# A mixture-of-experts layer on one core: its experts are worked two at a time, a wide one and a narrow one in turn

## The chip, the core and the metric

The kernel runs on one core of a Trainium2 chip. A core has a matrix engine (TensorE, PE), which multiplies a stationary operand of up to 128 x 128 (loaded by LDWEIGHTS, shown as PEld) with a moving one of up to 512 columns and adds up in PSUM; VectorE (DVE), ScalarE (ACT) and GpSimd (POOL) for elementwise work; and SyncE (SP), which here issues most DMAs. Sixteen DMA engines move data between DRAM and the on-chip memory SBUF. The metric is the device time of one execution in microseconds (us).

## What is computed

One layer over 1024 latent tokens of 1024 numbers, with a prefix of 256 context tokens: layer norm, a modulated branch of a state-space scan and window attention, a residual with layer norm, and a mixture of experts with a second residual and layer norm. The change lies in the experts. Each token goes to the 4 of 32 experts with the highest router value; an expert's rows are put through

```
def expert_block(args):
    xb, e = args
    gu = xb @ w_gate_up[e] + b_gate_up[e]          # 1024 x 2048
    glu, lin = jnp.split(gu, 2, axis=-1)
    glu = jnp.minimum(glu, SWIGLU_LIMIT)
    lin = jnp.clip(lin, -SWIGLU_LIMIT, SWIGLU_LIMIT)
    act = glu * jax.nn.sigmoid(SWIGLU_ALPHA * glu) * (lin + 1)
    return act @ w_down[e] + b_down[e]             # 1024 x 1024
```

and the result, times the token's gate, is added to the token's row. All is in float32; 12.6 MB of weights per expert come from DRAM.

## The kernel before, in words

Ahead of the experts the kernel ranks them by their number of rows (`ranks`, L1127). The expert of rank r gets room for `CAPS[r]` rows (L1059): 256 for the three fullest, then 240, 224, 208, four times 192, five times 160, and 128 for the other 17. Experts with more than 128 rows are *wide* and have two row blocks (`BLOCKS`), the 17 others are *narrow*. `ORDER` (L1061) takes ranks 0, 31, 1, 30, ..., so that a wide and a narrow expert alternate, down to the two last, 15 and 16, which are both narrow. Rows over the room would be done in a loop at the end (`rest`, L1707), which runs zero times here.

Each float32 product is made of three in a faster format (fp32r): a matrix is split into a high part (ACT copies it) and a low part (DVE subtracts), and high x high, low x high and high x low are added up. `Weights` (L1436) does this for the weights. An expert's weights come in 12 chunks of 1 MB, each as two halves with a DMA of their own (L1459, issued on SP) into one of 8 `raw` buffers (`P.ahead`); `prepare` copies each half to `wh` (ACT, L1476) and subtracts to `wl` (DVE, L1478). There are four pairs of split buffers, and the split runs three chunks ahead of PE, so the split of a step waits until PE has finished the chunk of the step before.

An expert is worked in 12 steps (`moe`, L1645), eight for the up projection and four for the down projection:

- `gather` fetches the expert's rows by an indirect DMA on POOL (L1240), with the lists that `places` (one-hot tables, DVE, L1182) and `slots` (small matmuls, L1198, and sums on DVE) made some steps before. `x_parts` (L1273) transposes four 128-column pieces of a block at a time on PE (`turn`, L1262) and splits them (`put`, L1269 and L1271) into `x`, of which there are two buffers.
- `up_wide` (L1333) has the weights stationary and the rows moving, so the result is already transposed; a chunk of 256 output columns takes two of the five PSUM accumulators (`K.mm`). `act_wide` (L1348) adds the bias, alternately for gate and linear columns, and writes `a` split.
- `up` (L1296), for narrow experts, has the rows stationary and 512 weight columns moving; two chunks make one accumulator, and after the second the bias is added by one more matmul (L1305): a stationary matrix `sel` of 64 rows that is one where the row is this expert's, times the table `K.bgu` of all experts' biases, 32 rows of high and 32 of low parts. `act` (L1317) makes the activation `um` in two halves; `turn` flips it (at steps 5 and 9, `TURN`) and `put` splits it into `a`.
- `down` (L1407) multiplies `a` with `w_down`: first the upper half of the rows of the weights for both halves of the output columns, then the lower half (`DOWN`, L1431). `store` (L1415) applies the gate (L1425) and adds the rows into `acc_d` by an indirect DMA on POOL (L1427), the first half of the columns at step 11 and the second at step 0 of the next expert.

In the loop the orders of PE, DVE and ACT are written out by hand: `tc.manual_schedule` keeps the instructions of its body in program order on each of them. `weave` takes turns among the jobs of a step: the last expert's store, this expert's activation, the next split, a part of the next expert's x. In each step come first the transposes of this step's x part and flip, then the woven jobs, then the products of the chunk (`main`). PSUM has eight buffers here: five accumulators, two for transposes (`K.tp`), one for the lists. A pool hands a buffer out anew when its last reader is done.

The lines that matter, from `moe`:

```
x = next(xs, None) if c in (1, 6, 7, 10) else None
cur.before(c)
weave(prev.store(1) if c == 0 and prev else None, cur.after(c), W.prepare(), x)
...
cur.main(c, W.ready.pop(0))
```

Of the kernel before, what the change touches and what calls it, by code (L numbers as in the profile page):

```python
# [8 lines left out]
F32 = mybir.dt.float32  # L9
# [10 lines left out]
D = 1024  # L20
# [1039 lines left out]
BLOCKS = {256: (128, 128), 240: (128, 112), 224: (128, 96), 208: (128, 80), 192: (128, 64), 160: (128, 32), 128: (128,), 64: (64,)}  # L1060
# [66 lines left out]
def ranks(tc, a, K):  # L1127
# [30 lines left out]
    v.tensor_copy(K.pick, K.pk.bitcast(F32))  # L1158
# [56 lines left out]
TURN = 5, 9  # L1215


class Expert:
# [4 lines left out]
    def __init__(self, tc, K, P, blocks, pick, lists, eid=None):  # L1223
        self.tc, self.nc, self.K, self.P, self.blocks, self.lists = tc, tc.nc, K, P, blocks, lists
        self.wide = len(blocks) == 2
        self.n = sum(blocks)
        self.pick = pick
        self.eid = eid
# [14 lines left out]
    def constants(self):  # L1243
        nc, P, K = self.nc, self.P, self.K
        if self.wide:
            nc.vector.tensor_scalar(self.bias[:, 8:16], self.bias[:, 8:16], 1.0, None, ALU.add)
        else:
            s = P.pk.tile([64, 256], F32R, tag="pk", name="pk")
            nc.vector.tensor_scalar(s, K.full, self.pick, None, ALU.mult)
            self.sel = s[:, 0:128] if self.n == 128 else s[:, 128:256]  # L1250

    def lo(self, b):

        return b * 128 + (256 if self.blocks[b] > 64 else self.blocks[b])
# [18 lines left out]
    def x_parts(self):  # L1273


        self.x = self.P.xt.tile([128, KT, 512], F32R, tag="x", name="x")
# [40 lines left out]
    def act(self, q):  # L1317
# [3 lines left out]
        x = self.whole(self.gu, nb, ("hg", "hu")[q])[0:nb]  # L1321
        t = P.tmp.tile([128, 512], F32, tag=("sg", "um")[q], name="t")[0:nb]
# [25 lines left out]
    def act_wide(self, c):  # L1348
# [4 lines left out]
        t = [P.tmp.tile([128, 512], F32, tag=("sg", "um")[q], name="t") for _ in range(2)]  # L1353
# [27 lines left out]
    def before(self, c):  # L1381
        if not self.wide and c in TURN:
            self.pt = self.turn(0, lambda i: self.um[0:self.n, i * 128:(i + 1) * 128])

    def after(self, c):

        if c == 1:
            self.a = self.P.at.tile([128, KT, 512], F32R, tag="a", name="a")
        if not self.wide and c in TURN:
            yield from self.put(self.a, TURN.index(c) * 4, 0, self.lo(0), self.pt)  # L1390
        if c == 11:
# [7 lines left out]
    def main(self, c, w):  # L1399
        if c >= 8:  # L1400
            self.down(c % 2, (c - 8) // 2 * 4, w)
# [29 lines left out]
DOWN = [("w_down", 4, k, c) for k in (0, 4) for c in (0, 512)]  # L1431
# [4 lines left out]
class Weights:  # L1436
# [133 lines left out]
def expert_consts(tc, a, K, late):  # L1570
    nc = tc.nc
    K.bgu = late.tile([64, 2 * D], F32R, name="bgu")
    K.full = late.tile([64, 256], F32, name="full")
    nc.gpsimd.memset(K.full, 1.0)
    nc.gpsimd.memset(K.full[:, 192:256], 0.0)
    br = K.wp.tile([128, KT, 256], F32, tag="raw", name="br").rearrange("p k n -> p (k n)")[0:64]
    for j in range(2):
        nc.sync.dma_start(out=br[j * 32:(j + 1) * 32], in_=a["b_gate_up"])
    nc.gpsimd.tensor_scalar(br[:, D:], br[:, D:], 1.0, 1.0, ALU.add, ALU.mult)
# [6 lines left out]
def moe(tc, a, K):  # L1586
    nc = tc.nc
    es = ExitStack()
    with es:
# [4 lines left out]
        with ExitStack() as st:  # L1594
            P = expert_pools(tc, a, K, st, True)
            W = Weights(tc, a, P)
            for r in ORDER:
                W.add(lambda r=r: expert_id(nc, K, r), CAPS[r] > 128)
# [3 lines left out]
            def expert_id(nc, K, r):  # L1602
                if r not in regs:
                    regs[r] = nc.sync.value_load((eid if P.ahead == 8 else K.eid)[0:1, r:r + 1], min_val=0, max_val=31)
# [12 lines left out]
            def start(i, ls):  # L1617
# [3 lines left out]
                e = Expert(tc, K, P, BLOCKS[CAPS[r]], K.pick[:, r:r + 1], ls, lambda: expert_id(nc, K, r))  # L1621
# [4 lines left out]
            with tc.manual_schedule(engines={mybir.EngineType.PE, mybir.EngineType.DVE, mybir.EngineType.Activation}):  # L1626
# [7 lines left out]
                P.ahead = 8  # L1634
# [5 lines left out]
                nxt = start(1, next(it))  # L1640
                weave(W.prepare())
                cur.constants()
            prev = None
            with tc.manual_schedule(engines={mybir.EngineType.PE, mybir.EngineType.DVE, mybir.EngineType.Activation}):
                for i in range(len(ORDER)):  # L1645
                    xs = iter(nxt.x_parts()) if nxt else iter(())
                    for c in range(12):
                        if c == 5:
                            ls = next(lists(i + 2, oh) or iter(()), None)
                        x = next(xs, None) if c in (1, 6, 7, 10) else None  # L1650
                        cur.before(c)
                        weave(prev.store(1) if c == 0 and prev else None, cur.after(c), W.prepare(), x)
                        if c == 2:
                            oh = place(i + 2)
                        if c == 8:
                            n2 = start(i + 2, ls)
                        if c == 10 and nxt:
                            nxt.constants()
                        cur.main(c, W.ready.pop(0))
                    prev, cur, nxt = cur, nxt, n2  # L1660
                weave(prev.store(1))
# [45 lines left out]
def rest(tc, a, K):  # L1707
    nc = tc.nc
    v = nc.vector
    with ExitStack() as es:  # L1710
# [4 lines left out]
        with tc.For_i(0, count, 1) as i:  # L1715
# [18 lines left out]
            pk = sm.tile([64, 1], F32, tag="pk", name="pk")  # L1734
            v.tensor_tensor(pk, K.route[0:64, 65:66], row[0:64, 33:34], ALU.is_equal)
            W = Weights(tc, a, P)
            W.add(eid)
# [6 lines left out]
            for c in range(12):  # L1744
                e.before(c)
                weave(e.after(c), W.prepare())
# [498 lines left out]
```

## Time and profile before

| | |
|---|---|
| Median of three runs | 2791.53 us (2789.71 to 2792.7) |
| Profiled execution | 2796.39 us, its span 2794.6 us |
| Mean granted TensorE clock | 0.943 of full speed |
| PE, PEld busy over the span | 2523.9 us (90%), 2123.3 us (76%) |
| DVE, ACT, POOL busy | 2234.2 us (80%), 1465.9 us (52%), 465.0 us (17%) |
| Read from DRAM, written | 551.76 MB, 76.57 MB |

The span runs from the first to the last instruction. The expert loop begins with the first product of an expert at 1149.5 us and ends with its last store at 2725.4 us. Matmuls overlap one another and their ends are modelled, so the sum of their durations says little; the step from one start to the next one's says what a product costs.

### The profile page before, as it was taken

To read this page: it belongs to the slowest core of one execution; us is meant where nothing else is said; L and a number is where in the kernel's file an instruction comes from. 1 tells how busy PE (TensorE), PEld (TensorE's weight loads), DVE (VectorE), ACT (ScalarE), POOL (GpSimd) and SP (SyncE) were. 2 spreads that over 40 slices of the span, in tenths; PEclk is the share of its full clock that TensorE was granted. 3 is DMA by queue.
4 is the path that set the end of the run, shared out by engine and by line. 5 is a ranking of instruction groups with operands and counts; after the bars stand their busy time and mean duration, and the time that the engine had idled before them with its cause. 6 is when DMAs were issued, how large, how long until landed. Compare 5 with 4: busy or idle time off the path is not lost. (4 is left out here: it accounts for less than half of the span.)

```text
span 2794.6 us, 41588 instructions
## 1 busy us (share of the span) xinstructions
PE 2523.9 (90%) x14030; PEld 2123.3 (76%) x14030; DVE 2234.2 (80%) x4306; ACT 1465.9 (52%) x2352; POOL 465.0 (17%) x303
## 2 busy tenths in 40 slices
PE   6799999978887877699999999999999999999990
PEld 1698887767686767588888888889888887888770
DVE  9636796347788887788878888888988899899995
ACT  0623113656555422455656666666666666666661
POOL 3200000034333243210110110110111011101113
PEclk8799999979998877699999999999999999999995
DMA  7434623554454463678979978988998999899983
GB/s 252 155 125 157 202 87 116 161 172 136 163 169 139 146 195 102 209 244 266 290 226 284 295 242 283 292 273 272 303 294 262 305 301 300 275 305 302 311 280 144
DMA packets 409674, 631.11 MB, mean 226 GB/s; under 512 B 36497, under 2 KB 215569, under 8 KB 408497
## 3 DMA queue, kind: packets, MB, share of 16 engines
q1 hardware_dynamic: 397152, 584.37, 63.8%
q0 software_dynamic: 11872, 42.47, 6.5%
q8 instruction: 112, 1.84, 0.3%
q10 hardware_dynamic: 432, 1.57, 0.2%
q14 instruction: 106, 0.86, 0.1%
HBM read 551.76 MB, written 76.57 MB: 225 GB/s over the span
## 5 line engine op out<-in xcount | busy, mean ns | idle before, releaser
L1478 DVE TENSOR_TENSOR wl<-raw,wh 128x1024 fp32r<-128x1024 f32 x768 | 920.8, 1219 | 163.4 <-ACT wh L1476 162.3
L1476 ACT ACTIVATE wh<-raw 128x1024 fp32r<-128x1024 f32 x768 | 790.3, 1052 | 246.5 <-PE dn L1294 87.9
L1344 PE MATMUL uw<-x,wh 128*128 128x320 f32 (+5 forms) x1920 | 581.3, 366 | 0.2 <-issue 0.2
L1345 PE MATMUL uw<-x,wl 128*128 128x192 f32 (+4 forms) x1920 | 501.4, 261 | 0.0
L1344 PEld LDWEIGHTS uw<-x,wh 128*128 128x128 f32 x1920 | 364.3, 190 | 24.0 <-issue 0.3
L1345 PEld LDWEIGHTS uw<-x,wl 128*128 128x128 f32 x1920 | 369.6, 193 | 0.5
L1291 PE MATMUL dn<-wh,a 128*128 128x512 f32 (+4 forms) x752 | 298.7, 397 | 0.0
L1292 PE MATMUL dn<-wl,a 128*128 128x512 f32 (+4 forms) x752 | 293.6, 390 | 0.0
L1427 POOL DMA_INDIRECT acc_d<-y,wi x47 | 120.4, 2562 | 958.3 <-DVE y L1425 816.3
L1294 PE MATMUL dn<-wh,a 128*128 128x512 f32 (+3 forms) x608 | 238.5, 392 | 0.6 <-DVE a L1271 0.6
L1291 PE MATMUL up<-wh,x 128*128 128x512 f32 x544 | 221.8, 408 | 0.0
L1294 PE MATMUL up<-wh,x 128*128 128x512 f32 x544 | 213.0, 392 | 0.0
L1292 PE MATMUL up<-wl,x 128*128 128x512 f32 x544 | 212.3, 390 | 0.0
L1356 ACT ACTIVATE t<-uw,bias 128x160 f32<-128x160 f32 (+5 forms) x240 | 98.6, 419 | 134.5 <-PE uw L1345 131.6
L1291 PEld LDWEIGHTS dn<-wh,a 128*128 128x128 f32 (+4 forms) x752 | 135.7, 180 | 37.8 <-issue 4.1
L1292 PEld LDWEIGHTS dn<-wl,a 128*128 128x128 f32 (+4 forms) x752 | 135.8, 181 | 33.9
L608 POOL TENSOR_SCALAR P<-P,su 128x640 f32<-128x640 f32 (+1 forms) x64 | 55.1, 874 | 608.0 <-DVE su L606 543.9
L1294 PEld LDWEIGHTS dn<-wh,a 128*128 128x128 f32 (+3 forms) x608 | 112.8, 186 | 28.4 <-DVE a L1271 2.7
L42 ACT ACTIVATE whi<-raw 128x2048 fp32r<-128x2048 f32 x38 | 72.8, 1917 | 112.9 <-PE mm L53 72.5
L1240 POOL DMA_INDIRECT x<-xm_d,ri x47 | 53.3, 1135 | 463.3 <-DVE L L1202 304.0
L1291 PEld LDWEIGHTS up<-wh,x 128*128 128x128 f32 x544 | 102.3, 188 | 27.4 <-issue 8.4
L1294 PEld LDWEIGHTS up<-wh,x 128*128 128x128 f32 x544 | 102.1, 188 | 22.4
(532 smaller groups left out, 5349.2 us busy)
## 6 DMA issues: line engine op xcount, KB each, us to landing
raw<-w_gate_up SPq DMA_DIRECT2D x512, 512.0 KB
raw<-w_down SPq DMA_DIRECT2D x256, 512.0 KB
mw<-w_mod SPq DMA_DIRECT2D x64, 256.0 KB
raw<-w_o SPq DMA_DIRECT2D x16, 1024.0 KB
raw<-w_in SPq DMA_DIRECT2D x13, 1024.0 KB
raw<-w_mod SPq DMA_DIRECT2D x8, 1024.0 KB
gate_d<-gs SPq DMA_DIRECT2D x16, 512.0 KB
raw<-w_att_out SPq DMA_DIRECT2D x8, 1024.0 KB
```

What stands on the lines that cost most here:

```text
L42: nc.scalar.activation(out=hi, in_=src, func=ACTF.Copy)
L608: nc.gpsimd.tensor_scalar(P[i][:, 0:nl + 256], P[i][:, 0:nl + 256], su[:, 0, i:i + 1], 1.0, ALU.mult, ALU.mult)
L1240: nc.gpsimd.indirect_dma_start(out=x[0:nb], out_offset=None, in_=K.xm_d, bounds_check=S - 1, oob_is_err=True, in_offset=bass.IndirectOffse ...
L1291: nc.tensor.matmul(ps, lhsT=h, rhs=wh[:, k], start=st, stop=False)
L1292: nc.tensor.matmul(ps, lhsT=h, rhs=wl[:, k], start=False, stop=en and nb <= 64)
L1294: nc.tensor.matmul(ps, lhsT=X[:, k0 + k, lo:lo + nb], rhs=wh[:, k], start=False, stop=en)
L1344: nc.tensor.matmul(p[:, 0:2 * n], lhsT=wh[:, k, fs], rhs=self.x[:, k, 0:2 * n], start=k == 0, stop=False)
L1345: nc.tensor.matmul(p[:, 0:m], lhsT=wl[:, k, fs], rhs=self.x[:, k, 0:m], start=False, stop=k == KT - 1)
L1356: nc.scalar.activation(out=y[i], in_=self.uw[i][:, 1], func=ACTF.Identity, bias=self.bias[:, q * 8 + j0 + i:q * 8 + j0 + i + 1])
L1427: nc.gpsimd.indirect_dma_start(out=K.acc_d, out_offset=bass.IndirectOffsetOnAxis(ap=wi[0:nb], axis=0), in_=o[0:nb], in_offset=None, bounds ...
L1476: nc.scalar.activation(out=h, in_=r, func=ACTF.Copy)
L1478: nc.vector.tensor_tensor(l, r, h, ALU.subtract)
```

## The change

Two experts of `ORDER` are worked together, in 24 steps: chunk c of the first, chunk c of the second, chunk c + 1 of the first, and so on. The weights are fetched in that order. Of the two, the first has side 0 and the second side 1, and `x`, `a` and the temporaries have buffers of their own for each side; there is one `x` per side instead of two that all share, and six raw halves instead of eight. The down projection goes by output columns: both halves of the rows for columns 0 to 511, then for 512 to 1023, with `store(0)` at step 10. The parts of the next pair's x are made in the down steps (`PARTS`), those of the second expert of the first pair in the very first step. The flip comes in the step after the activation's, whosever it is. `sel` and `K.bgu` get 128 rows, of which the lower 64 are zero.

```diff
-BLOCKS = {..., 128: (128,), 64: (64,)}
+BLOCKS = {..., 128: (128,)}
...
-    K.pick = late.tile([64, 32], F32, name="pick")
+    K.pick = late.tile([128, 32], F32, name="pick")
+    v.memset(K.pick[64:128], 0.0)
...
-TURN = 5, 9
+FLIP = 4, 8
+PLACE = (1, 0), (4, 0)
+LISTS = (2, 0), (5, 0)
+GATHER = (3, 1), (6, 1)
+PARTS = (8, 0), (8, 1), (9, 1), (10, 0), (10, 1), (11, 0)
...
-            s = P.pk.tile([64, 256], F32R, tag="pk", name="pk")
-            nc.vector.tensor_scalar(s, K.full, self.pick, None, ALU.mult)
-            self.sel = s[:, 0:128] if self.n == 128 else s[:, 128:256]
+            self.sel = P.pk.tile([128, 128], F32R, tag="pk", name="pk")
+            nc.vector.tensor_scalar(self.sel, K.full, self.pick, None, ALU.mult)
...
+    def big(self, pool, tag):
+        return pool.tile([128, KT, 256 if self.side else 512], F32R, tag=tag + "AB"[self.side], name=tag)
+    def tmp(self, tag):
+        return self.P.tmp.tile([128, 512], F32, tag=tag + "AB"[self.side], bufs=1 if self.side else 2, name="t")
...
-    def before(self, c):
-        if not self.wide and c in TURN:
-            self.pt = self.turn(0, lambda i: self.um[0:self.n, i * 128:(i + 1) * 128])
+    def flip(self):
+        p = self.turn(0, lambda i: self.um[0:self.n, i * 128:(i + 1) * 128])
+        self.flips += 1
+        return self.put(self.a, self.flips * 4 - 4, 0, self.lo(0), p)
...
-        if c == 11:
+        if c == 10:
             yield from self.store(0)
...
-            self.down(c % 2, (c - 8) // 2 * 4, w)
+            self.down((c - 8) // 2, c % 2 * 4, w)
...
-DOWN = [("w_down", 4, k, c) for k in (0, 4) for c in (0, 512)]
+DOWN = [("w_down", 4, k, c) for c in (0, 512) for k in (0, 4)]
...
-    def add(self, eid, wide=False):
-        for m, kn, k, c in WIDE if wide else CHUNKS:
-            self.todo += [(eid, m, kn // 2, k + i * kn // 2, c) for i in range(2)]
+    def add(self, *experts):
+        for cs in zip(*(WIDE if wide else CHUNKS for _, wide in experts)):
+            for (eid, _), (m, kn, k, c) in zip(experts, cs):
+                self.todo += [(eid, m, kn // 2, k + i * kn // 2, c) for i in range(2)]
...
-    P.ahead = 8 if deep else 4
+    P.ahead = 6 if deep else 4
-    P.row = pool("erow", 2)
-    P.xt = pool("ext", 2 if deep else 1)
+    P.row = pool("erow", 3)
+    P.xt = pool("ext", 1)
-    P.y = pool("ey", 2)
+    P.y = pool("ey", 3)
...
-    K.bgu = late.tile([64, 2 * D], F32R, name="bgu")
-    K.full = late.tile([64, 256], F32, name="full")
+    K.bgu = late.tile([128, 2 * D], F32R, name="bgu")
+    K.full = late.tile([128, 128], F32, name="full")
+    nc.gpsimd.memset(br[64:128], 0.0)
...
-                for i in range(len(ORDER)):
-                    xs = iter(nxt.x_parts()) if nxt else iter(())
-                    for c in range(12):
-                        ...
+                for i in range(2, len(ORDER) + 2, 2):
+                    more = i < len(ORDER)
+                    for c, s in ((c, s) for c in range(12) for s in range(2)):
+                        e = cur[s]
+                        put = flip.flip() if flip else None
+                        if (c, s) in LISTS:
+                            ls = next(lists(i + LISTS.index((c, s)), oh) or iter(()), None)
+                        if (c, s) == PARTS[0] and more:
+                            xs = itertools.chain(*(n.x_parts() for n in nxt))
+                        x = next(xs, None) if (c, s) in PARTS or (c, s) == (0, 0) else None
+                        y = next(xs, None) if (c, s) == (0, 0) else None
+                        weave(prev[s].store(1) if c == 0 and prev else None, e.after(c), W.prepare(), put, x, y)
+                        if (c, s) in PLACE:
+                            oh = place(i + PLACE.index((c, s)))
+                        if (c, s) in GATHER:
+                            n = GATHER.index((c, s))
+                            nxt = (nxt if n else ()) + (start(i + n, ls),)
+                        if c == 10 and more:
+                            nxt[s].constants()
+                        e.main(c, W.ready.pop(0))
+                        flip = e if not e.wide and c in FLIP else None
+                    prev, cur = cur, nxt
+                for e in prev:
+                    weave(e.store(1))
```

## Rows read from the trace of the kernel before

**Rows 1.** The page's slices: busy tenths in 40 equal slices of the span.
```profile
PE   6799999978887877699999999999999999999990
```

**Rows 2.** Windows: stretch, length, busy us (instructions) of each engine, PEclk, DMA share, GB/s.
```profile
1149.50:2725.50 1576.00, 1563.24 (x8508) 1320.21 (x8508) 1383.72 (x2530) 1002.99 (x1424) 169.87 (x91) 0.99 0.89 280
2185.40:2279.10 93.70, 93.39 (x542) 79.06 (x541) 85.53 (x166) 62.23 (x92) 11.71 (x6) 1.00 0.94 298
2239.60:2279.10 39.50, 39.19 (x182) 30.21 (x181) 38.22 (x57) 27.92 (x33) 6.87 (x3) 1.00 1.01 321
```

**Rows 3.** Waits, 1270 to 2651 us: total us, times, longest.
```profile
PE tp L1262 <- DVE t L1330: 3.9, 13, 0.3
...
ACT wh L1476 <- DMA raw<-w_gate_up: 1.3, 4, 0.6
```

**Rows 4.** Timeline of PE around a bias product: start us, us, instruction.
```profile
2245.33 0.39 PE L1294 MATMUL up<-wh,x 128*128 128x512 f32 x1
2245.64 0.49 PE L1305 MATMUL up<-bgu,pk 64*128 64x512 f32 x1
2246.07 0.50 PE L1291 MATMUL up<-wh,x 128*128 128x512 f32 x1
2246.40 0.39 PE L1292 MATMUL up<-wl,x 128*128 128x512 f32 x1
2246.63 0.40 PE L1294 MATMUL up<-wh,x 128*128 128x512 f32 x1
```

**Rows 5.** Timeline of the weight loads (PEld) in the same stretch.
```profile
2245.64 0.18 PEld L1305 LDWEIGHTS up<-bgu,pk 64*128 64x128 f32 x1 [0.35 <-issue]
...
2246.17 0.19 PEld L1292 LDWEIGHTS up<-wl,x 128*128 128x128 f32 x1
```

**Rows 6.** Timeline of PE before transposes of 32 rows.
```profile
2262.52 0.39 PE L1294 MATMUL up<-wh,x 128*128 128x512 f32 x1
2262.84 0.62 PE L1262 MATMUL tp<-ident,x 32*128 32x32 f32 x4
```

**Rows 7.** All instructions of L1305: duration ns (min/median/max), first and last start, forms.
```profile
L1305 PE MATMUL up<-bgu,pk x68: 492/492/492, 1236.1 to 2713.3; 64*128 64x512 f32 x68
```

**Rows 8.** DVE's groups, 2185.4 to 2279.1 us: busy us, mean ns, idle before.
```profile
L1478 DVE TENSOR_TENSOR wl<-raw,wh 128x1024 fp32r<-128x1024 f32 x48 | 57.6, 1218 | 7.7 <-ACT wh L1476 7.7
L1358 DVE TENSOR_TENSOR t<-uw,t 128x160 f32<-128x160 f32 x16 | 4.4, 315 | 0.0
...
L1326 DVE TENSOR_TENSOR t<-up,t 128x512 f32<-128x512 f32 x2 | 1.4, 683 | 0.0
```

**Rows 9.** Timelines of PE, DVE and POOL at the loop's start, by time.
```profile
1146.90 1.97 PE L1262 MATMUL tp<-ident,x 128*128 128x128 f32 x8 [8.03 <-DVE x L1271]
1153.38 1.39 DVE L1182 TENSOR_SCALAR oh<-iota,posr 128x128 bf16<-128x128 bf16 x8
1155.79 0.40 PE L1344 MATMUL uw<-x,wh 128*128 128x512 f32 x1
1156.13 0.39 PE L1344 MATMUL uw<-x,wh 128*128 128x512 f32 x1
1159.65 1.80 POOL L1240 DMA_INDIRECT x<-xm_d,ri  x1 [23.74 <-DVE gt L1211]
1166.08 1.12 PE L1262 MATMUL tp<-ident,x 128*128 128x128 f32 x4 [7.23 <-DMA x<-xm_d,ri]
1166.85 0.77 PE L1344 MATMUL uw<-x,wh 128*128 128x512 f32 x1
```

**Rows 10.** Waits of POOL's scatters for one another, 1270 to 2651 us.
```profile
POOL acc_d L1427 <- DMA acc_d<-y,wi: 31.3, 4, 8.6
```

**Rows 11.** Timeline of POOL at the loop's end.
```profile
2726.45 1.55 POOL L1427 DMA_INDIRECT acc_d<-y,wi  x1 [29.19 <-DVE ei L1699]
```

**Rows 12.** Windows, after the last scatter (columns as in rows 2).
```profile
2733.00:2736.00 3.00, 0.00 (x0) 0.00 (x0) 0.00 (x0) 0.00 (x0) 0.00 (x0) 0.50 0.00 0
```

**Rows 13.** The page's costliest groups: the high parts of the weights.
```profile
L1476 ACT ACTIVATE wh<-raw 128x1024 fp32r<-128x1024 f32 x768 | 790.3, 1052 | 246.5 <-PE dn L1294 87.9
```

More of the change, by code (lines that the diff above doesn't have):

```diff
@@ L1 @@
+import itertools
 import math
@@ L1273, in x_parts @@
     def x_parts(self):
-        self.x = self.P.xt.tile([128, KT, 512], F32R, tag="x", name="x")
+        self.x = self.big(self.P.xt, "x")
         for b in range(len(self.blocks)):
@@ L1320, in act @@
         nc, P, nb = self.nc, self.P, self.n
[L1321 to L1322 removed]
+        x = self.gu[0:nb]
+        t = self.tmp(("sg", "um")[q])[0:nb]
         if q == 0:
@@ L1352, in act_wide @@
         q, j0 = c % 2, c // 2 * 2
-        t = [P.tmp.tile([128, 512], F32, tag=("sg", "um")[q], name="t") for _ in range(2)]
+        t = [self.tmp(("sg", "um")[q]) for _ in range(2)]
         x, y = [a[:, 0:n] for a in t], [a[:, 256:256 + n] for a in t]
@@ L1379, in act_wide @@
                 v.tensor_tensor(self.a[:, j0 + i, lo:lo + m], x[i][:, k:k + m], hi[:, k:k + m], ALU.subtract)
-    def before(self, c):
-        if not self.wide and c in TURN:
-            self.pt = self.turn(0, lambda i: self.um[0:self.n, i * 128:(i + 1) * 128])
+    def flip(self):
+        p = self.turn(0, lambda i: self.um[0:self.n, i * 128:(i + 1) * 128])
+        self.flips += 1
+        return self.put(self.a, self.flips * 4 - 4, 0, self.lo(0), p)
     def after(self, c):
         if c == 1:
-            self.a = self.P.at.tile([128, KT, 512], F32R, tag="a", name="a")
-        if not self.wide and c in TURN:
-            yield from self.put(self.a, TURN.index(c) * 4, 0, self.lo(0), self.pt)
-        if c == 11:
+            self.a = self.big(self.P.at, "a")
+        if c == 10:
             yield from self.store(0)
@@ L1571, in expert_consts @@
     nc = tc.nc
-    K.bgu = late.tile([64, 2 * D], F32R, name="bgu")
-    K.full = late.tile([64, 256], F32, name="full")
+    K.bgu = late.tile([128, 2 * D], F32R, name="bgu")
+    K.full = late.tile([128, 128], F32, name="full")
     nc.gpsimd.memset(K.full, 1.0)
-    nc.gpsimd.memset(K.full[:, 192:256], 0.0)
-    br = K.wp.tile([128, KT, 256], F32, tag="raw", name="br").rearrange("p k n -> p (k n)")[0:64]
+    br = K.wp.tile([128, KT, 256], F32, tag="raw", name="br").rearrange("p k n -> p (k n)")
+    nc.gpsimd.memset(br[64:128], 0.0)
     for j in range(2):
         nc.sync.dma_start(out=br[j * 32:(j + 1) * 32], in_=a["b_gate_up"])
-    nc.gpsimd.tensor_scalar(br[:, D:], br[:, D:], 1.0, 1.0, ALU.add, ALU.mult)
+    nc.gpsimd.tensor_scalar(br[0:64, D:], br[0:64, D:], 1.0, 1.0, ALU.add, ALU.mult)
     for c in range(4):
@@ L1596, in moe @@
             W = Weights(tc, a, P)
-            for r in ORDER:
-                W.add(lambda r=r: expert_id(nc, K, r), CAPS[r] > 128)
+            for i in range(0, 32, 2):
+                W.add(*((lambda r=r: expert_id(nc, K, r), CAPS[r] > 128) for r in ORDER[i:i + 2]))
             regs = {}
@@ L1633, in moe @@
                 regs.clear()
-                P.ahead = 8
+                P.ahead = 6
                 for x in cur.x_parts():
@@ L1639, in moe @@
                 it = lists(1, place(1))
-                nxt = start(1, next(it))
+                cur = cur, start(1, next(it))
                 weave(W.prepare())
-                cur.constants()
-            prev = None
+                for e in cur:
+                    e.constants()
+            prev = flip = None
+            xs = iter(cur[1].x_parts())
             with tc.manual_schedule(engines={mybir.EngineType.PE, mybir.EngineType.DVE, mybir.EngineType.Activation}):
-                for i in range(len(ORDER)):
-                    xs = iter(nxt.x_parts()) if nxt else iter(())
-                    for c in range(12):
[L1648 to L1661, printed above, removed]
@@ L1733, in rest @@
             v.tensor_copy(inf[:, :, 3:6], K.info[:, :, 0, 3:6])
-            pk = sm.tile([64, 1], F32, tag="pk", name="pk")
-            v.tensor_tensor(pk, K.route[0:64, 65:66], row[0:64, 33:34], ALU.is_equal)
+            pk = sm.tile([128, 1], F32, tag="pk", name="pk")
+            v.memset(pk[64:128], 0.0)
+            v.tensor_tensor(pk[0:64], K.route[0:64, 65:66], row[0:64, 33:34], ALU.is_equal)
             W = Weights(tc, a, P)
-            W.add(eid)
+            W.add((eid, False))
             e = Expert(tc, K, P, (128,), pk, next(slots(tc, K, P.li, K.lg, places(tc, K, P.li, lambda t: pos[:, t:t + 1], 128),
@@ L1744, in rest @@
             for c in range(12):
-                e.before(c)
-                weave(e.after(c), W.prepare())
+                weave(e.after(c), W.prepare(), e.flip() if c - 1 in FLIP else None)
                 e.main(c, W.ready.pop(0))
```

14 lines of the change are left out of this document (8 added, 6 removed).

## The prediction, made before the change was run

> **What bounds the kernel now.** I read the page's slices first, to find the stage that the change touches: in the last 24 of the 40 slices TensorE (PE) stands at nine tenths nearly throughout [rows 1]. A high share leaves open whether PE works or is fed just in time, so I read the expert loop next, in one row, for a late pair of a wide and a narrow expert, and for the narrow one alone [rows 2]. Over the loop PE is busy 1563.24 of 1576.00 us. In the late pair PE is busy 93.39 of 93.70 us, VectorE (DVE) 85.53, ScalarE (ACT) 62.23, the DMA engines 0.94 of the time. So PE is the bound, and DVE and DMA have 6 to 9% to spare. The waits say it from the other side: between 1270 and 2651 us PE waits 3.9 us for a transpose's input, and the longest entry of ACT waiting for up weights from DRAM is 1.3 us in four waits [rows 3]. Two consequences: evening out DMA and DVE over a pair wins nothing by itself, because PE starves in neither half of a pair; and a wait that the new order puts into PE's queue costs its full length.
>
> Last I looked for time inside PE's stream that isn't work: the step from one matmul's start to the next one's. A 512-column product follows its predecessor by 0.23 us (2246.40 to 2246.63). Around the bias product with 64 rows (L1305) the steps are longer [rows 4]: 2245.33 to 2245.64 (0.31), to 2246.07 (0.43), to 2246.40 (0.33). The weight loads show why: that of L1292 starts at 2246.17, while the matmul that started at 2246.07 still streams, but that of L1305 starts only with its own matmul, after 0.35 us in which the loader was idle [rows 5]. The row that separates "few rows" from another reason is the x transposes with 32 rows: entering them takes 0.32 us as well (2262.52 to 2262.84) [rows 6].
>
> **The change, part by part.**
>
> *Bias products with 128 rows.* Three steps of together 1.07 us (2245.33 to 2246.40) become three of 0.23, together 0.69: 0.38 us less. There are 68 such products, all of 492 ns [rows 7], four in each of 17 narrow experts, all in the PE-bound loop: 68 x 0.38 = 26 us. From below: if the stretch has a reason that stays, 0, or a loss, should a load of 128 rows take 0.01 us more than one of 64 (0.19 and 0.18 [rows 5]), of 68 x 0.01 = 0.7 us. I take 26, since the 32-row transposes show the same entry and the 128-row neighbours don't. The zeros in the extra rows are written once ahead of the loop: 0.
>
> *Two experts in turn.* Matmuls, transposes, weight splits, gathers and scatters are the same in number and shape; what can change is who waits. PE meets four conditions:
> - Weights. The split runs three chunks ahead of PE before and after; the raw buffers go from eight halves to six. A pair has 48 halves, so one lasts 93.7/48 = 1.95 us and the lead shrinks by 3.9 us. The split chunks stand between, 3 x 93.7/24 = 11.7 us of PE's time, and ACT hardly waits for DRAM now [rows 3]. 0; from above it is the 3.9 us once a pair, 16 x 3.9 = 62 us, if every pair's burst of gathers and scatters used up the rest.
> - DVE's pace. 85.5 us per late pair stand against 93.7 - 4 x 0.38 = 92.2 of PE. 57.6 of the 85.5 are splits [rows 8], 2.4 a step; the other 28 are uneven. A wide step with the second half of an activation has fourteen short instructions of some 0.2 to 0.3 us (the adds 0.3 [rows 8]), with the split about 5.5 us, and PE's wide step takes (93.7 - 39.5)/12 = 4.5; a narrow step that only splits has 2.4 in 39.5/12 = 3.3. Added up step by step, DVE falls behind by at most some 3 us around the fourth and fifth chunk, is level again at the seventh, and does the same over the down chunks, where x parts, the narrow flip and the stores come together.
> - The narrow flip. Its input (L1330) is written in the narrow step and transposed ahead of the next wide one. With that lag it is ready some 1 us before PE comes there, at the fourth chunk about level. PE pays for this very wait now: 3.9 us in 13 waits [rows 3].
> - Accumulators. A wide chunk takes two of the five buffers, a narrow one holds one over two chunks. When the narrow product of chunk 2, 4 or 6 needs one, the wide pair of the chunk before was read by the adds at the start of the wide step: about 3 us to spare.
> By this working the waits are near 0, but with 0 to 1 us of margin at two or three places in a pair: 0 to 1.5 us a pair, 0 to 24 us. I take 0.3 for each of 16 pairs, the size of the wait of today: +5 us.
>
> *Down projection by columns.* The same products. Half of the columns are done after the second down chunk, so a wide expert holds two accumulators at a time instead of four; with four there would be none for the narrow one. 0.
>
> *x single-buffered.* The parts of the next pair are made in the down chunks, when x was read for the last time, from rows gathered four chunks earlier, so nothing is left for a pair's first step. For the first pair it is: both parts of the second expert now stand ahead of the first product in PE's order. Before, PE did chunk 0, waited 7.23 us for the gather until 1166.08, transposed, and began chunk 1 at 1166.85 [rows 9]. The gather was issued at 1159.65, behind sums of selection matmuls that were mixed in with chunk 0, though their one-hot table was ready at 1153.38 + 1.39 = 1154.8. With PE idle the gather goes about 3 us earlier and lands at about 1163. Eight transposes of a PE that comes from a wait took 1.97 us (1146.90), so chunk 0 starts at about 1165. PE then has chunk 0 to do, sixteen times the 0.34 us from 1155.79 to 1156.13, and one part less, 0.77 us from 1166.08 to 1166.85 and about half of that at full pace: 1165 + 5.5 - 0.4 - 1166.85 = +3.3, and some 0.7 more (an estimate) because PE runs slowly after the longer wait. +4 us (+1 if the rows land 3 us sooner still, +8 if they land no sooner than now).
>
> *The tail.* Both last experts now end together. The first one's scatter-add can go one narrow chunk (12 products of 0.23, 2.8 us) before the second one's, which has to wait for it: scatters into the accumulator wait for each other (31.3 us in four waits [rows 10]). From its issue at 2726.45 [rows 11] the last one's transfers took until at the latest 2733, from where the DMA engines are idle [rows 12]: 6.5 us. The second goes that long after the first instead of 2.8: 6.5 - 2.8 = +3.7 us (0 if they overlap, +7.8 with the mean wait of rows 10, 31.3/4).
>
> *Sum*, on the profiled execution's own 2796.4 us (its span is 2794.6): -26 + 5 + 4 + 3.7 = -13.3, so 2783.1. The median of the runs is 2791.5, 4.9 below the profiled one: 2778.
>
> **The rivals.**
> *The accumulators come round to the same buffer (slower).* 2 + 1 + 2 is five, the number of buffers. Handed out strictly in turn, the narrow product of chunks 2 and 6 gets the very buffer that the previous one left. Its last reader (L1326) stands in DVE's queue behind the first half of a split, and that split waits for the weight buffer that PE frees with the chunk just done. PE then waits for one wh copy, one wl and the multiply, 1.05 + 1.22 + 0.68 = 2.95 us [rows 8, 13], twice in each of 15 pairs: 89 us, 2867 at worst. From 13.3/30 = 0.45 us a wait on, the kernel is slower than before. For it: the trace doesn't show which buffer a product gets. Against it: the wide pair's buffers are free by then, and only a fixed order would pass them over. The Trainium skill, "Perfetto Trace Analysis" (Optimization Strategy), says that a gap repeating on the engine that should be saturated can mean too few PSUM buffers for the next tile; no run here shows it yet. Several smaller waits for DVE, above 1.1 us a pair in all, end in the same place. 13%.
> *The bias products stay slow (slower).* Then +12.7 remains: 2804. For it: nothing in the trace shows this product with 128 rows. Against it: rows 4 to 6. 5%. The Trainium skill, "TensorE: Matmul & The Clock Gate" (The mechanism), says that a weight load overlaps a running matmul only when it goes to another row group; by that, full-height loads don't overlap and 128 rows win nothing. The loads here do start under the matmul before [rows 5]: the trace doesn't agree.
> *The small waits eat the gain (no change).* At 0.8 to 1.4 us a pair instead of 0.3 the sum lies between -5.5 and +4: 2786 to 2796. DVE at 0.93 of PE's time speaks for it; that it was busy 38.22 of 39.50 us in a narrow expert [rows 2] without holding PE up speaks against. 17%.
> *More than forecast.* No new wait and a start at +1: -26 + 1 + 3.7, 2770. It lies within the forecast.
>
> **How the numbers follow.** A measurement of this kernel tells about 0.2% (5.6 us) from no change: 2786 to 2797. The forecast, 2766 to 2786 with 2778 as its likeliest, gets 65%, no change 17%, slower 18% (13 + 5). The range takes in the no-change case and the second rival's lower part at the top, and the waitless case less 7 us, half a per cent of the loop, for gains not seen here at the bottom: 2763 to 2800.
>
> **What would show it.** L1305 with 128 rows, a step of 0.23 us and no idle loader before it; one wait of PE of about 13 us at the start, ahead of the first uw product; two scatters at the end, the second waiting for the first; waits of PE in the loop below 0.5 us a pair. Wrong: PE waiting microseconds for L1326 or L1330 at each second narrow chunk, ACT waiting for raw weights in the pairs, or L1305 still followed by 0.43 us.

## The result and the profile after

The changed kernel takes 2835.8 us (median of 4 runs, 2832.1 to 2838.2) beside 2790.6 for the kernel before on the same chip: a ratio of 1.0163 (95% interval 1.0145 to 1.0181). It is slower by some 45 us, and the prediction was 13 us faster. The profiled execution took 2838.2 us, its span 2836.2.

Page, the slices that answer to [rows 1], with the granted clock: TensorE (PE) still looks full.

```profile
PE   6799999978878777799999999999999999999990
...
PEclk8799999989998877899999999999999999999995
```

The loop in one window (columns as in [rows 2]; from the first product to the last):

```profile
1158.00:2767.00 1609.00, 1560.13 (x8495) 1345.10 (x8493) 1377.09 (x2502) 1002.40 (x1418) 151.84 (x90) 0.98 0.87 272
```

It is 33 us longer than in [rows 2], for the same products. That understates it: the window of before holds the 7.2 us in which PE waits for the first gather [rows 9], and here that wait lies ahead of the first product. From the first product behind the wide expert's chunk 0 (1166.85 us before, 1165.62 here) to the end of the last one it is 1558.5 us before and 1601.1 here, 42.6 more, though here both x parts of the narrow expert are done by then and before only one. In the window PE is idle for 49 us instead of 13 (of which 7.2 are that wait), and its mean granted clock is 0.98 instead of 0.99. The waits name both ends of the cause (1270 to 2651 us, as in [rows 3]):

```profile
ACT wh L1492 <- DMA raw<-w_gate_up: 57.0, 42, 4.1
PE tp L1276 <- DVE t L1344: 43.4, 14, 4.8
```

Before, these two stood at 1.3 and 3.9 us. Nearly all of PE's waiting in the loop is now in front of one instruction: the transposes of the first narrow flip, at step (5,0), which need the product um of VectorE (DVE, L1344) from step (4,1). Over the whole loop (from 1170 us on):

```profile
PE tp L1276 <- DVE t L1344: 46.8, 16, 4.8
```

One of these waits, in a late pair, read backwards: PE, then DVE, then ScalarE (ACT), then GpSimd.

```profile
2235.63 0.39 PE L1308 MATMUL up<-wh,x 128*128 128x512 f32 x1
2240.87 1.11 PE L1276 MATMUL tp<-ident,t 128*128 128x128 f32 x4 [4.85 <-DVE t L1344]
```

```profile
2231.41 1.23 DVE L1494 TENSOR_TENSOR wl<-raw,wh 128x1024 fp32r<-128x1024 f32 x1
2236.35 1.23 DVE L1494 TENSOR_TENSOR wl<-raw,wh 128x1024 fp32r<-128x1024 f32 x1 [3.72 <-ACT wh L1492]
2237.49 0.69 DVE L1393 TENSOR_TENSOR a<-t,a 128x128 fp32r<-128x128 f32 x4
2238.10 1.39 DVE L1184 TENSOR_SCALAR oh<-iota,posr 128x128 bf16<-128x128 bf16 x8
2239.40 0.69 DVE L1343 TENSOR_SCALAR t<-up 128x512 f32<-128x512 f32 x1
2240.12 0.69 DVE L1344 SCALAR_TENSOR_TENSOR t<-t 128x512 f32<-128x512 f32 x1
```

```profile
2231.29 0.57 ACT L1388 ACTIVATE a<-t 128x160 fp32r<-128x160 f32 x2 [1.27 <-DVE t L1385]
2235.26 1.06 ACT L1492 ACTIVATE wh<-raw 128x1024 fp32r<-128x1024 f32 x1 [3.39 <-DMA raw<-w_gate_up]
```

```profile
2202.59 2.94 POOL L1441 DMA_INDIRECT acc_d<-y,wi  x1 [56.65 <-DVE y L1439]
2213.88 2.23 POOL L1441 DMA_INDIRECT acc_d<-y,wi  x1 [8.35 <-DVE wl L1494]
2222.35 1.82 POOL L1441 DMA_INDIRECT acc_d<-y,wi  x1 [6.25 <-DVE a L1393]
2224.48 1.08 POOL L1249 DMA_INDIRECT x<-xm_d,ri  x1 [0.30 <-DVE wl L1494]
2225.86 1.05 POOL L1249 DMA_INDIRECT x<-xm_d,ri  x1 [0.30 <-issue]
```

A pair's three scatter-adds now come together and go one after the other, some 10 us each, and the next wide expert's gathers stand right behind the third. (The view names DVE instructions on `wl` and `a` ahead of the second and third, but a scatter-add reads neither; in e5 below the same wait is put down to the scatter-add before.) SyncE asks for a half of the weights at the moment of the first gather:

```profile
2224.50 0.37 SPq L1475 DMA_DIRECT2D raw<-w_gate_up  x1
```

Counted in order, this is the half that ACT gets only at 2235.26, 10.8 us later; the one asked for at 2222.76 was there for a copy at 2228.96, 6.2 us later. DVE's queue is in order, so the split waits 3.72 us, and the activation's sums, the one-hot table and um stand behind it.

What the DMA engines and the clock do there (columns as in [rows 2]):

```profile
2216.00:2222.00 6.00, 6.00 (x39) 5.47 (x38) 5.61 (x22) 3.79 (x6) 0.10 (x1) 1.00 0.89 254
...
2224.00:2235.00 11.00, 11.00 (x71) 10.15 (x71) 8.41 (x16) 5.62 (x10) 2.30 (x3) 1.00 1.05 294
2236.00:2240.80 4.80, 0.02 (x1) 0.00 (x0) 4.41 (x16) 3.96 (x6) 0.00 (x0) 0.97 1.07 364
2241.00:2247.80 6.80, 6.80 (x37) 6.74 (x38) 6.44 (x15) 2.12 (x4) 1.05 (x1) 0.53 0.75 236
2248.00:2252.00 4.00, 4.00 (x23) 3.44 (x23) 2.32 (x3) 2.89 (x5) 0.00 (x0) 1.00 0.76 280
```

The DMA share is full from 2224 to 2240.8. And the wait is paid again: after PE stood idle for 4.85 us its granted clock is 0.53 on the mean of the next 6.8 us, nearly all at the lower level (0.5, 1.2 GHz). PE is busy throughout, but a pair of the wide step's products takes 0.48 us at this level and 0.26 behind it:

```profile
2242.61 0.52 PE L1358 MATMUL uw<-x,wh 128*128 128x320 f32 x1
...
2243.09 0.52 PE L1358 MATMUL uw<-x,wh 128*128 128x320 f32 x1
...
2247.66 0.33 PE L1358 MATMUL uw<-x,wh 128*128 128x320 f32 x1
...
2247.92 0.34 PE L1358 MATMUL uw<-x,wh 128*128 128x320 f32 x1
```

The part of the change that was to win did so. The bias product (L1319) in PE's and the weight loader's timeline, answering to [rows 4, 5]:

```profile
2228.53 0.40 PE L1308 MATMUL up<-wh,x 128*128 128x512 f32 x1
2228.76 0.40 PE L1319 MATMUL up<-bgu,pk 128*128 128x512 f32 x1
2228.99 0.30 PE L1358 MATMUL uw<-x,wh 128*128 128x320 f32 x1
```

```profile
2228.53 0.19 PEld L1319 LDWEIGHTS up<-bgu,pk 128*128 128x128 f32 x1
```

Steps of 0.23 us, and the load runs under the product before.

### The profile page after: what moved, and what is told of

The parts are those of the page before. It is cut to its first block, busy times and chain, and to the rows that moved or that the text cites. A ratio compares the mean times of both kernels' runs of the same rounds, so it can differ in the third digit from the quotient of the medians.

```text
span 2836.2 us, 41774 instructions
## 1 busy us (share of the span) xinstructions
PE 2524.7 (89%) x14030; PEld 2152.3 (76%) x14030; DVE 2243.5 (79%) x4307; ACT 1471.2 (52%) x2352; POOL 452.8 (16%) x303
## 4 chain that ended last, share of the span: by engine, by line
PE 41%; DVE 8%; DMA 7%; ACT 2%; issue 1%; POOL 0%; POOLq 0%; SPq 0%; DVEq 0%; ACTq 0%
PE uw L1358 9%; PE dn L1305 6%; PE dn L1306 6%; DMA raw<-w_gate_up 6%; PE dn L1308 5%; PE uw L1359 4%; PE up L1305 2%; DVE wl L1494 2%; PE up L1308 2%; PE up L1306 2%; PE tp L1276 2%; ACT wh L1492 2%; DVE oh L1184 1%; PE sl L1200 1%; DVE a L1393 1%
## 5 line engine op out<-in xcount | busy, mean ns | idle before, releaser
L1358 PE MATMUL uw<-x,wh 128*128 128x320 f32 (+5 forms) x1920 | 598.0, 372 | 0.0
L1358 PEld LDWEIGHTS uw<-x,wh 128*128 128x128 f32 x1920 | 373.7, 195 | 26.8
L1359 PEld LDWEIGHTS uw<-x,wl 128*128 128x128 f32 x1920 | 378.6, 197 | 3.6
L1305 PE MATMUL dn<-wh,a 128*128 128x512 f32 x752 | 304.5, 405 | 0.0
L1306 PE MATMUL dn<-wl,a 128*128 128x512 f32 x752 | 294.2, 391 | 0.0
L1441 POOL DMA_INDIRECT acc_d<-y,wi x47 | 102.9, 2190 | 1141.6 <-DVE y L1439 814.3
L1305 PE MATMUL up<-wh,x 128*128 128x512 f32 x544 | 216.2, 397 | 0.1
L1306 PEld LDWEIGHTS dn<-wl,a 128*128 128x128 f32 x752 | 136.5, 181 | 32.6
L1305 PEld LDWEIGHTS dn<-wh,a 128*128 128x128 f32 x752 | 136.4, 181 | 32.1
L1305 PEld LDWEIGHTS up<-wh,x 128*128 128x128 f32 x544 | 102.7, 189 | 19.2 <-PE uw L1359 0.3
L1306 PEld LDWEIGHTS up<-wl,x 128*128 128x128 f32 x544 | 103.0, 189 | 17.7
L52 PE MATMUL mm<-whi,uh 128*128 128x256 f32 x320 | 108.4, 339 | 4.5 <-DVE r L307 4.5
```

The costliest lines, as they stand in the source:

```text
L52: nc.tensor.matmul(out, lhsT=lsel(lh, k), rhs=rsel(rh, k), start=start and k == 0, stop=False)
L1305: nc.tensor.matmul(ps, lhsT=h, rhs=wh[:, k], start=st, stop=False)
L1306: nc.tensor.matmul(ps, lhsT=h, rhs=wl[:, k], start=False, stop=en and nb <= 64)
L1358: nc.tensor.matmul(p[:, 0:2 * n], lhsT=wh[:, k, fs], rhs=self.x[:, k, 0:2 * n], start=k == 0, stop=False)
L1359: nc.tensor.matmul(p[:, 0:m], lhsT=wl[:, k, fs], rhs=self.x[:, k, 0:m], start=False, stop=k == KT - 1)
L1441: nc.gpsimd.indirect_dma_start(out=K.acc_d, out_offset=bass.IndirectOffsetOnAxis(ap=wi[0:nb], axis=0), in_=o[0:nb], in_offset=None, bounds ...
```

## The experiments

The stretch ahead of the loop differs between executions (five profiles with the loop order of before start the loop at 1133.9 to 1149.5 us), so beside each ratio I give the loop's own length in the profile, from its first product to the end of its last: 1575.9 us before, 1608.5 after. Such lengths come from one profile each, and they compare only kernels of one order, because of the first gather's wait (above).

Theory A: the lead of six raw halves doesn't outlast the burst of scatter-adds and gathers; the split is late, and um behind it. Theory B: DVE's own work around the fourth chunk makes um late, and the DRAM waits are a by-product. C: DVE is late for everything, and PE would wait elsewhere if not for the flip.

**e1: the kernel before, bias products with 128 rows.**

```
-    K.bgu = late.tile([64, 2 * D], F32R, name="bgu")
+    K.bgu = late.tile([128, 2 * D], F32R, name="bgu")
...
+            self.sel = P.pk.tile([128, 128], F32R, tag="pk", name="pk")
```

> The kernel before with one part of the change: bias products with 128 rows, the 64 new ones zero. If my term is right, each product of 0.43 us becomes a step of 0.23 and the steps beside it go back to 0.23: 68 x 0.38 = 26 us less, 2765 us beside 2791. Rival: DVE, at 0.93 of PE's time, takes the gain back as waits of PE for weights or transposes: 2785 to 2791. Second rival: the steps stay at 0.32 and 0.42: 2791.

Ratio 0.9976 (0.9961 to 0.9991), 2783.2 us; the loop 1567.6. The steps are 0.23, as expected, but only 8 of the 26 us arrive. That is close to the rival (2785 to 2791), and by its mechanism: PE waits ahead of transposes, though not for weights. PE's waits in the loop, and the same narrow expert as in [rows 2]:

```profile
PE tp L1262 <- DVE t L1330: 23.0, 30, 1.1
```

```profile
2231.40:2270.50 39.10, 37.77 (x182) 30.49 (x182) 38.23 (x57) 27.93 (x33) 6.09 (x3) 1.00 1.01 316
```

PE needs 1.42 us less than the 39.19 of before, DVE its 38.23 as ever, and the expert ends only 0.40 sooner. DVE, busy for 38.23 of 39.10 us, sets the pace of a narrow expert now.

**e2: the kernel before with six halves.**

```
-    P.ahead = 8 if deep else 4
+    P.ahead = 6 if deep else 4
```

> The kernel before with six halves of raw weights instead of eight, in its own order. Theory A (the smaller lead doesn't cover the burst of scatter-adds and gathers, so weights are split late and what stands behind the splits on DVE is late): ACT waits for raw up weights well above the 1.3 us of before, 10 to 60 us in the loop; PE hardly feels it in the old order, where the narrow flip had a lists product and more steps ahead of it: 2791 to 2800. Theory B (DVE's own work around the fourth chunk is what makes the flip late, the DRAM waits are a by-product): ACT's waits stay below 5 us and the time at 2791.

Ratio 1.0014 (0.9996 to 1.0032), 2793.6 us; the loop 1580.5, 5 us longer. ACT waits for up and down weights:

```profile
ACT wh L1476 <- DMA raw<-w_gate_up: 59.3, 72, 3.7
ACT wh L1476 <- DMA raw<-w_down: 39.0, 61, 2.2
```

That is more than in the changed kernel, and from 1170 us on PE waits 9.7 us in all instead of 4.8. So late weights by themselves cost little here; they cost where an input of PE stands close behind them.

**e3: the changed kernel with eight halves.** The one-hot table `o` now lies in the gates' tile, dead by then.

> The changed kernel with eight halves of raw weights again; room for them comes from one-hot tables, gates and a sum put into buffers that are idle then, and nothing else moves. Theory A: ACT's waits for raw up weights fall from 57 us to below 10, PE's waits for the narrow flip from 46.8 to below 10, and the dips of the clock that follow them go too: 2835 - 47 - 15 = about 2774. Theory B: the flip's waits stay above 30 us, 2820 or more.

```
-    P.ahead = 6 if deep else 4
+    P.ahead = 8 if deep else 4
...
-    o = pool.tile([128, 8, 256], BF16, tag="oh", bufs=1, name="oh")
+    o = o.bitcast(BF16).rearrange("p (t n) -> p t n", t=8)
...
-        t = P.tmp.tile([64, 512], F32, tag=tag, bufs=1, name=tag)[0:nb]
+        t = P.tmp.tile([128, 512], F32, tag="sgA", bufs=2, name="t")[0:nb]
```

Ratio 0.9946 (0.9928 to 0.9964), 2776.2 us. Waits, as in [rows 3], and the loop:

```profile
PE tp L1277 <- DVE t L1345: 9.4, 11, 1.5
```

```profile
ACT wh L1493 <- DMA raw<-w_gate_up: 6.7, 11, 1.3
```

```profile
1159.70:2706.70 1547.00, 1534.62 (x8494) 1321.86 (x8492) 1372.85 (x2502) 999.89 (x1418) 159.24 (x90) 1.00 0.89 283
```

Theory A by its numbers. B falls as the main cause; of the flip's waits 10.6 us are left over the loop, with hardly a wait for DRAM beside them. In these two profiles the missing halves cost 62.0 us of loop (1609.0 - 1547.0): PE is idle 36.5 us less here (12.4 instead of 48.9), and busy 25.5 us less (1534.62 instead of 1560.13) for the same products. The clock accounts for the latter: after the loop's start the granted clock drops to 0.5 fourteen times, 68.3 us together, in the changed kernel, and twice, 6.8 us together, here. With the loop's first microseconds PE is busy at that level for 65.5 us there and 10.7 here; at half speed that makes some 27 us of difference (an estimate).

**e10: e3's other edits, with six halves.** The two lines on `P.ahead` are undone.

> The changed kernel with the edits that made room for eight halves (one-hot tables, gates and a sum in buffers that are idle then) but with six halves. If the lead is what mattered: 2836, flip waits near 47 us, as without these edits. Rival: the edits themselves changed the order or freed a wait: below 2815.

Ratio 1.0130 (1.0107 to 1.0152), 2832.8 us. The profile is that of its slowest execution (2849.4):

```profile
PE tp L1277 <- DVE t L1345: 59.2, 18, 5.8
```

The lead did it, not the edits. By the ratios it is worth 51 us (e10 against e3) to 61 us (the changed kernel against e3).

**e4: the changed kernel, the first flip one step later.**

```
-                        flip = e if not e.wide and c in FLIP else None
+                        if not e.wide and c in FLIP:
+                            due[(c + 1, s) if c == 4 else (c + s, 1 - s)] = e
```

> The changed kernel with the first flip of a narrow expert one step later: ahead of its own fifth chunk instead of the wide one's. Theories A and B both let the flip's waits go from 46.8 us to below 5, if three chunks of split weights (11.7 us) cover DVE's lag: about 2774. Rival C: DVE is late for everything, so PE waits for wl, wh or the put instead: 2815 or more. ACT's waits for raw up weights stay at some 57 us by A, since nothing in the DMA queues is moved.

Ratio 1.0095 (1.0078 to 1.0112), 2816.9 us, the loop 1584.6. A miss: 24 of the 62 us.

```profile
PE sl L1200 <- DVE oh L1184: 19.2, 12, 2.4
PE tp L1276 <- DVE t L1344: 4.2, 1, 4.2
```

The flip no longer waits, but the next of PE's instructions that needs DVE does, the lists product at (5,0), for the one-hot table. The time is C's (2815 or more), and C holds in part: it is the whole of DVE's queue that is late there. But no wait of PE, here or in another run, is put down to split weights, which have three chunks of lead.

**e6: the changed kernel, the second one-hot table at (2,1).**

```
-PLACE = (1, 0), (4, 0)
+PLACE = (1, 0), (2, 1)
```

> The changed kernel with the second one-hot table (1.39 us of DVE) made at (2,1) instead of (4,0), where it stands in DVE's queue ahead of the product um. If DVE's queue alone sets the flip, each of 16 waits shrinks by 1.39 us or goes: 46.8 to about 26 us, and with fewer dips of the clock about 2808. If the flip is late by the DRAM wait alone and DVE idles ahead of it, the same 1.39 us come off, because the table stands behind the late split; below 2800 or above 2825 would speak against both.

Ratio 1.0087 (1.0062 to 1.0113), 2817.2 us, the loop 1587.3; flip waits 35.1 us in 14 instead of 46.8 in 16. The direction that both theories gave, about half the size expected for the waits.

**e5: the changed kernel, the gathers one or two steps later.**

```
-GATHER = (3, 1), (6, 1)
+GATHER = (4, 1), (7, 0)
```

> The changed kernel, still with six halves, its two gathers one or two steps later: at (4,1) and (7,0) instead of (3,1) and (6,1). If the lead is short only while a gather and the scatter-adds ahead of it hold the DMA engines, ACT still waits for raw up weights (40 us or more in the loop), but later than the product um of the fourth chunk: PE's waits for the first flip fall from 46.8 to below 15 us, about 2790. Rival: the scatter-adds and the weights alone hold the DMA engines long enough: the flip still waits over 30 us, 2820 or more.

Ratio 1.0173 (1.0153 to 1.0194), 2838.9 us, flip waits 48.8 us in 18. That is the rival's outcome, but it tests neither side, since the gather did not move. GpSimd's timeline shows it:

```profile
2188.44 2.94 POOL L1441 DMA_INDIRECT acc_d<-y,wi  x1 [56.75 <-DVE y L1439]
2199.24 2.72 POOL L1441 DMA_INDIRECT acc_d<-y,wi  x1 [7.87 <-DMA acc_d<-y,wi]
...
2210.33 1.08 POOL L1249 DMA_INDIRECT x<-xm_d,ri  x1 [0.30 <-DVE wl L1494]
```

21.89 us from the first scatter-add to the gather, as in the changed kernel (2202.59 to 2224.48). Both stand in GpSimd's own queue, and what held the gather was the third scatter-add, not its line in the program.

**e9: the gather held back by its lists.**

```
-PLACE = (1, 0), (4, 0)
-LISTS = (2, 0), (5, 0)
-GATHER = (3, 1), (6, 1)
+PLACE = (1, 0), (5, 1)
+LISTS = (5, 0), (6, 1)
+GATHER = (5, 1), (7, 0)
```

> The changed kernel, six halves, with the lists of the next wide expert made at (5,0), behind the first flip, its gather issued from (5,1), and the narrow one's table, lists and gather at (5,1), (6,1) and (7,0). Moving the gather's place in the program alone did nothing, because GpSimd ran it at the same moment, right behind the third scatter-add; now its lists hold it back until the flip is done. If the gather on top of the scatter-adds makes the splits late for the fourth chunk: flip waits from 46.8 us (35.1 with the table alone moved) to below 12, about 2785. Rival: the three scatter-adds alone already use up a lead of six halves: 30 us or more, about 2815.

Ratio 0.9920 (0.9897 to 0.9943), 2771.7 us, with six halves. The flip (PE) now stands ahead of the gather (POOL), which comes 15.9 us after the last scatter-add:

```profile
2195.59 0.60 PE L1276 MATMUL tp<-ident,t 128*128 128x128 f32 x4
```

```profile
2183.41 1.90 POOL L1441 DMA_INDIRECT acc_d<-y,wi  x1 [5.66 <-DVE t L1340]
2199.27 1.08 POOL L1249 DMA_INDIRECT x<-xm_d,ri  x1 [13.96 <-DVE L L1204]
```

```profile
PE tp L1276 <- DVE t L1344: 5.2, 5, 2.9
ACT wh L1492 <- DMA raw<-w_gate_up: 20.9, 24, 4.0
```

ACT's waits stood at 67.1 over the loop in the changed kernel. With the gather out of the way six halves do as well as eight (2776.2 us in e3), so the lead is short where gather and scatter-adds meet. The edit also takes a table (e6: 11.7 us of waits) and the list sums (some 2 us of DVE) from ahead of um; what these did to the flip waits was not separated.

**e8 and e11: e1 with the first flip at chunk 6,** in e11 also with the x part of chunk 6 at chunk 5.

```
-TURN = 5, 9
+TURN = 6, 9
...
-                        x = next(xs, None) if c in (1, 6, 7, 10) else None
+                        x = next(xs, None) if c in (1, 5, 7, 10) else None
```

> The kernel before with bias products of 128 rows and the first flip of a narrow expert at chunk 6 instead of 5. The 128 rows alone left PE waiting 23 us for flips, and the time fell by 7 instead of 26. If these waits are what took the gain back, the first flips' 15.5 us go: about 2769. Rival: DVE can't keep PE's new pace in a narrow expert (38 of 39.5 us busy before, now 38 of 38), and PE waits for wl, wh or the second flip instead: 2783.

> The kernel before with 128-row bias products, the first narrow flip at chunk 6, and the x part of chunk 6 at chunk 5, since flip and x part in one chunk wait for each other's transpose buffer (22.5 us). If the flips' waits are what took the gain of the 128 rows back, PE's waits fall below 10 us and the time to about 2772. Rival: in a narrow expert DVE has no time left, and the waits come back at another place: 2783 or more.

e8: 1.0015 (1.0000 to 1.0029), the gain gone: flip and x part in one chunk wait for the two transpose buffers (22.5 us in 14). e11: 0.9953 (0.9935 to 0.9971), 2780.9 us, loop 1566.5, a miss (2772 expected). From 1170 us on PE waits 24.0 us, as in e1 (23.6), now 17.1 for flips and 6.6 for x parts. In the old order DVE's 38 us per narrow expert come back wherever PE next needs DVE.

**e7: the edits of e3, e4 and e6 together.**

> The changed kernel with eight halves, the first flip one step later and the second one-hot table at (2,1), so that neither the flip nor the lists product stands close behind DVE. PE's waits fall from 10.6 + 1.7 us to below 4: 2776 - 9 = about 2767. Rival: DVE is then late for wl, and the waits come back there: 2776.

Ratio 0.9910 (0.9894 to 0.9926), 2765.6 us, the fastest: PE idle 4.8 us in a loop of 1536.7.

**e12: e7 with bias products of 64 rows.**

```
-            nc.tensor.matmul(p, lhsT=self.sel, rhs=K.bgu[:, c0:c0 + 512], start=False, stop=True)
+            nc.tensor.matmul(p, lhsT=self.sel[0:64], rhs=K.bgu[0:64, c0:c0 + 512], start=False, stop=True)
```

> The changed kernel with eight halves, late flip and early table, and the bias products back to 64 rows: the one that measures the bias term where PE waits for nothing. My term: 68 x 0.38 = 26 us more, 2766 + 26 = 2792, as slow as the kernel before. Rival: the longer steps hide under waits that are there anyway: 2766 to 2775.

Ratio 0.9983 (0.9971 to 0.9994), 2787.0 us. The loops of e7 and e12:

```profile
1156.40:2693.10 1536.70, 1531.86 (x8494) 1319.56 (x8492) 1372.36 (x2501) 990.87 (x1418) 155.47 (x90) 1.00 0.90 284
```

```profile
1160.90:2720.20 1559.30, 1558.74 (x8494) 1319.72 (x8492) 1374.68 (x2501) 996.80 (x1418) 152.61 (x90) 0.99 0.89 280
```

PE's busy time differs by 26.9 us and the loop by 22.6, since the 4.8 us of waits in e7 are nearly gone here. Up to 4.5 of the 26.9 us are clock (PE is at 0.5 for 16.4 us of this loop and 7.3 of e7's). The steps into, at and behind the 68 bias products add up to 65.9 us here and 41.9 in e7, 24.0 apart. The medians are 21 us apart, 26 expected.

## Why the prediction was wrong

The step that failed is *Weights*, "0; from above it is the 3.9 us once a pair, 16 x 3.9 = 62 us". The two halves cost 62.0 us of loop (after against e3). That this meets the upper bound is chance: the mechanism isn't PE missing weights. The lead shrank as reckoned: from the request for a half to its copy on ACT it is 13.4 us at the median before and 9.7 in the changed kernel (1270 to 2651 us, counted in order), 3.7 less, while a half in the burst above took 10.8. I counted the split chunks (three, 11.7 us) as cover, and they are one for PE's products. But a late half also stops DVE's queue, in which um stands, and um has a step of cover, not three. I had checked the lead and the flip's margin each by itself: the flip with DVE "by at most some 3 us" behind, the lead with ACT that "hardly waits for DRAM now". The second was true with eight halves, and the first assumed it. What [rows 3] could have told: ACT waited little, but how early the halves lay there it doesn't show. And the waits cost 1.7 times their length (62.0 for 36.5), by the clock; I had priced a wait at its length. Of the signs that I had named for being wrong, ACT's waits for raw weights came. The first rival's last line, several smaller waits for DVE above 1.1 us a pair, named the outcome (46.8/16 = 2.9 us a pair) without its cause.

The other terms, point by point:
- *Bias, -26.* The size is about right (24.0 us in the steps of PE, e12 against e7), the place not: in the order of before only 8.3 us of loop arrive (e1), since a narrow expert left DVE 1.28 us [rows 2], and four faster bias products take 4 x 0.38 = 1.52 from PE's side. So "evening out DMA and DVE over a pair wins nothing by itself" holds (e12, 0.9983), but the two parts need each other: 128 rows alone give 0.9976, both with the lead kept 0.9946, and 0.9910 with the margins mended. The Trainium skill, "Perfetto Trace Analysis" (Optimization Strategy), says that where the busiest engine changes over time, interleaving the stretches may help. The runs agree once the 128 rows had made DVE the bound of the narrow stretch (2783.2 us in e1, 2765.6 in e7); with 64 rows it won next to nothing (e12).
- *Waits for DVE, +5.* With eight halves the flips' waits are 10.6 us over the loop instead of 4.2: +6.4 in place of 5, within its bounds.
- *Accumulators.* In the changed kernel no wait of PE in the loop is put down to a reader of an accumulator, and the most in any run is 2.6 us (four waits in e9, for L1340); that rival is out.
- *Bias stays slow.* Out. The Trainium skill, "TensorE: Matmul & The Clock Gate" (The mechanism), says that a weight load overlaps a running matmul only when it goes to another row group; the trace doesn't agree, since loads of 128 rows start under the running product (2228.53 above).
- *Start, +4.* PE waited 6.99 us for the gather, not some 13:

```profile
1156.59 1.97 PE L1276 MATMUL tp<-ident,x 128*128 128x128 f32 x8 [6.99 <-DMA x<-xm_d,ri]
1158.21 0.77 PE L1358 MATMUL uw<-x,wh 128*128 128x512 f32 x1
```

  The wide chunk 0 ends at 1165.62, all x parts done, where before PE stood at that point at 1166.85 [rows 9]. In this pair of executions it is -1.2. Over all profiles that point lies at 1163.7 us on the mean in the new order (nine, standard deviation 3.0) and at 1159.8 in the old (five, 5.9): +3.9, which fits the forecast, but the spread leaves the size open.
- *Tail, +3.7.* The scatter-adds go 6.9 us apart (I had 6.5), yet the tail from the last product on is 69.5 us against 69.2:

```profile
2765.07 1.58 POOL L1441 DMA_INDIRECT acc_d<-y,wi  x1 [53.12 <-DVE iq L1715]
2771.96 1.55 POOL L1441 DMA_INDIRECT acc_d<-y,wi  x1 [5.32 <-DMA acc_d<-y,wi]
```

  The sums are read back from 2781.77 on, 15.1 us after the last product; before it was 2740.88, 15.5 after, though the DMA engines had been idle since 2733 [rows 12]. Some 8 us of another wait covered it, which I hadn't looked for.

With *Weights* at its old lead the sum would have stood: 2776.2 us measured in e3, 2778 forecast. That it is so close is in part luck, since the tail's +3.7 did not come and the bias came out some 2 us smaller.

## What to carry to other kernels

A prefetch buffer is cover for everything behind the copy in the same engine's queue, so price a shorter lead at the most urgent instruction in that queue, not at the consumer of the data. When a change brings bursts together (three scatter-adds and a gather here), look at the time from request to use of the transfers that run beside them. And price a wait of several microseconds on PE together with the slower clock that follows it (here 1.7 times the wait).

## What the runs showed that was not expected

- PE's granted clock fell to 0.5 in or right behind 12 of the 13 flip waits of 1.9 us and more in the changed kernel; against e3, 36.5 us of idle time came with 25.5 us more busy time. Behind the waits of 1.2 us at 1308 and 1734 it stayed at 1.00. Of the other two of the fourteen drops, one (2749) came with a 1.7 us wait of another product and one (2019) with no wait of PE near it.
- Moving the issuing line of a gather by one or two steps moved it by nothing (21.89 us behind the first scatter-add in both); it ran right behind the third scatter-add in GpSimd's queue.
- Six instead of eight buffers cost 5 us of loop in one order of the same work (e2, its time not clear of no change) and 62 in another.
